# A hybrid decoder step on one core: the loads of the S5 constants moved from SyncE's order into ScalarE's

## The chip, the cores and the metric

The kernel runs on one core of a Trainium2 chip. The metric is device time in microseconds. Three runs of the kernel before gave 2245.57, 2238.49 and 2242.0 us, median 2242.0.

The engines are called by the profile's names: PE (TensorE matmul), PEld (TensorE weight load), DVE (VectorE), ACT (ScalarE), POOL (GpSimd), SP (SyncE). SP computes nothing; its instructions begin DMAs.

## The reference

One inference step of a trunk of 2 layers over a prompt of 2048 tokens, with 8 more single tokens (the "sample") through the same weights. In every layer the 1024 channels are split in four groups of 256, one a mixer: A (retention), H (gated linear recurrence), S (S5, a diagonal complex state space) and M (Mamba-2). All read one input projection, and an output projection and the residual end the layer:

```python
hn = rms_norm(x, norm_w)
proj = (hn @ w_in).astype(f32)
...
sy, s5_re, s5_im = s5_scan(u, s5_h0_re, s5_h0_im, s5_A_re, s5_A_im, s5_log_dt, s5_B_re, s5_B_im, s5_C_re, s5_C_im)
...
mixed = jnp.concatenate([o_ret, o_hgrn, o_s5, o_m2], axis=-1)
x_out = x + mixed @ w_out
```

## The kernel before, in words

**Tiling.** The prompt is cut in 4 blocks of 512 tokens. With 2 layers this makes 8 blocks, here called blocks 1 to 8 (1 to 4 are layer 0). A block's large matmuls (`gemm`, `gemm_wide`) multiply its normalised input by weight tiles of 256 KB. A weight tile goes through four engines: SP begins its load into a `wr` buffer (6 of them; lines 612 and 687), ACT makes a rounded copy in a `wh` buffer (5 of them; lines 615 and 688), DVE subtracts that copy from the raw tile for the rest (lines 616 and 689), and PE multiplies by both halves (lines 628, 633 and 695). The mixers' smaller work stands between these matmuls.

**S5.** `s5_setup` computes for each layer seven constant arrays of 512 KB in HBM, `s5c[l][0..6]`. In every block `mix_S` loads them again into `big` buffers (512 KB each; `NBIG` = 10 of them, shared with the other mixers, with the sample's work and with the gates). Eleven loads a block, 88 in all:

- `s5_load` (line 241) for arrays 0 and 1 (called `binc`) and 6 (`tcs`): 3 loads of 512 KB. Arrays 0 and 1 are read by PE's 64 matmuls of line 1420, array 6 by DVE's multiplications right behind. Eight ACT copies (line 1413) fill the other operand of line 1420, `uT`, from two transposes.
- `s5_out(0)` and `s5_out(1)` (lines 1425 and 1426): 4 loads of 256 KB each, two into `tq` and two into `cq`. PE's two groups of 32 matmuls (line 1482) read them, group 0 those of `s5_out(0)`, group 1 those of `s5_out(1)`; 12 matmuls of a large product stand between the two groups. After each group ACT copies the result out (line 1483).

In blocks 1 and 5 (`B.b` is 0) `s5_out(1)` is called after group 0, in the other blocks before it:

```python
tq, cq = nxt
if qh == 0 and B.b:
    nxt = s5_out(1)
elif qh == 1:
    if not B.b:
        tq, cq = s5_out(1)
    yield 1
```

**The sample's work.** In the second half of block 1 and 5 and the first of block 2 and 6 the 8 sample tokens go through their own mixers (class `Dec`), which use `big` buffers too. `Dec.mix_S` loads one with 16 small broadcasts a layer (line 1025, SP) and multiplies it into another (line 1030, DVE, twice).

**What sets the order.** PE's order is written out by hand: `tc.manual_schedule` keeps PE in the order in which the program is traced. On ACT, DVE, POOL and SP a scheduler of the framework sets the order when the program is built. It goes by priority, which is the position in the trace less the offset of `tc.high_priority` (the loads, casts and subtractions of weight tiles have 100, evacuations of large products 100, the sample's work minus 50), and by its own estimate of when inputs, buffers and engines are free. At run time every engine takes its instructions strictly in that order, and an instruction that begins a DMA waits in it like any other: for its buffer to be free, and for one earlier DMA to have landed (DMAs are counted on eight semaphores in turn). In the kernel before all 1284 DMAs are begun by SP.

Of the kernel before, what the change touches and what calls it, by code (L numbers as in the profile page):

```python
# [113 lines left out]
def trunk_kernel(ctx: ExitStack, tc: tile.TileContext, A: dict):  # L114
    nc = tc.nc
# [34 lines left out]
    def big(shape=(P, 1024), dt=F32):  # L150
        if alt[0] and AB[alt[0]]:
            return smp.tile(list(shape), dt, name=nm("big"), tag="big" + alt[0], bufs=AB[alt[0]])
        return bigp.tile(list(shape), dt, name=nm("big"), tag="big")
# [83 lines left out]
    s5c = [[drp.tile([P, 1024], F32, name=f"s5c{i}_{j}", tag=f"s5c{i}_{j}") for j in range(7)] for i in range(DEPTH)]  # L237

    def s5_load(l, j):
        t = big()  # L240
        nc.sync.dma_start(t, s5c[l][j])
        return t

    hA = hH = hM = None
# [1153 lines left out]
    def mix_S(L, B):  # L1398
# [5 lines left out]
        for hb in range(2):  # L1404
            ps = mbank()
            for i in range(4):
                g = hb * 8 + 2 * i
# [3 lines left out]
            for g2, sg in halves():  # L1411
                for r, sl in halves():
                    (V.tensor_copy if 2 * r + g2 in UV else S.copy)(uv[sl, :, g2, :], pv[sg, :, r, :])
        binc = [s5_load(L.l, j).rearrange("p (a q x) -> p a q x", a=2, q=4) for j in range(2)]
        yield 3
        bre, bim = mbank(), mbank()
# [5 lines left out]
        def s5_out(qh):  # L1422
            tq, cq = big([P, 2, 4, P]), big([P, 2, 4, P])
            for hb in range(2):
                nc.sync.dma_start(tq[:, hb], s5c[L.l][2 + hb][:, 512 * qh : 512 * qh + 512].rearrange("p (g x) -> p g x", g=4))
                nc.sync.dma_start(cq[:, hb], s5c[L.l][4 + hb][:, 512 * qh : 512 * qh + 512].rearrange("p (g x) -> p g x", g=4))
            return tq, cq

        tcs = s5_load(L.l, 6).rearrange("p (a q j) -> p a q j", a=2, q=8)
        tc_ = tcs[:, 0].rearrange("p q j -> p (q j)")  # L1430
        ts_ = tcs[:, 1].rearrange("p q j -> p (q j)")
# [29 lines left out]
        carry = cn  # L1461
        yield 4
        nxt = s5_out(0)
        Y = big([P, 8, P])
        yield 4
        for qh in range(2):
# [7 lines that stand above are left out]
            ps = mbank()  # L1474
            for q2 in range(2):
                for r in range(2):
                    g4 = 2 * q2 + r
                    for i in range(2):
                        for hb in range(2):
                            q = 4 * hb + 2 * qh + q2  # L1480
                            lhs = uT[:, 2 * q + r, :] if i else X[:, r, q, :]
                            T.matmul(ps[64 * hb : 64 * hb + 64, g4 * P : (g4 + 1) * P], lhs, (tq if i else cq)[:, hb, g4], start=(i == 0), stop=(i == 1))  # L1482
            S.copy(Y[:, :, qh * 64 : qh * 64 + 64].rearrange("p t (g c) -> p g t c", g=4), ps.rearrange("p (g t c) -> p g t c", g=4, c=16))
# [404 lines left out]
    for l in range(DEPTH):  # L1888
        L = Layer()
# [163 lines left out]
```

## Time and profile before

| what | value |
|---|---|
| three runs | 2245.57, 2238.49, 2242.0 us; median 2242.0 |
| the profiled execution's own time | 2245.02 us |
| its span, first to last instruction | 2243.2 us |
| mean granted TensorE clock | 0.98 of full speed |
| PE busy | 2118.9 us (94%) |
| DVE busy | 1669.3 us (74%) |
| ACT busy | 1034.2 us (46%) |
| POOL busy | 239.5 us (11%) |
| DMA | 284.41 MB, mean 127 GB/s |

The profile is one execution. "Busy" counts the engines' own work; waits and the beginning of DMAs are not in it, so SP has no busy time. A timeline row is: start in us, length in us, engine and line, operation, the tile written and the tiles read, the shapes, how many instructions were merged; in square brackets the idle time before it and what ended it. A small "q" behind an engine's name is its sequencer. A matmul's end is modelled.

### The profile page before, as it was taken

The numbers are of one execution on the slowest core, as the hardware profiler recorded it, in microseconds if no ns is written. First come the engines' busy times: TensorE is split into PE (matmuls) and PEld (weight loads), VectorE is DVE, ScalarE is ACT, GpSimd is POOL, SyncE is SP. The second block draws the span as 40 slices with busy tenths as digits, with TensorE's granted clock in tenths as the row PEclk, the third lists the DMA queues.
The fourth block names the chain that finished last, engine by engine and source line by source line (L and its number), as shares of the span: only waits on it lengthen the run. The fifth ranks groups of instructions, "written<-read, shape, count | busy, mean of one in ns | idle before, by whom it ended". The sixth has DMA issues, their size and how long they took to land. (4 is left out here: it accounts for less than half of the span.)

```text
span 2243.2 us, 41062 instructions
## 1 busy us (share of the span) xinstructions
PE 2118.9 (94%) x15031; PEld 1712.8 (76%) x15031; DVE 1669.3 (74%) x4614; ACT 1034.2 (46%) x1889; POOL 239.5 (11%) x212
## 2 busy tenths in 40 slices
PE   7999989999999999999999998999899899999996
PEld 7778767776777877788877876777677678878786
DVE  6888666898749977787747867489985687748774
ACT  7434433456333564346453453444634245454343
POOL 0112011000210002201100011000120001100100
PEclk9999999999999999999999999999999999999999
DMA  6324633236524364374533335334652253431272
GB/s 213 104 66 120 182 104 118 90 108 203 143 67 143 94 196 121 115 167 126 179 97 112 95 113 165 99 109 119 202 154 78 86 163 101 156 92 50 68 260 94
DMA packets 263354, 284.41 MB, mean 127 GB/s; under 512 B 88752, under 2 KB 183616, under 8 KB 263152
## 3 DMA queue, kind: packets, MB, share of 16 engines
q1 hardware_dynamic: 263152, 281.79, 42.4%
q8 instruction: 118, 1.93, 0.4%
q14 instruction: 84, 0.69, 0.1%
HBM read 245.52 MB, written 31.99 MB: 124 GB/s over the span
## 5 line engine op out<-in xcount | busy, mean ns | idle before, releaser
L695 PE MATMUL gb<-wh,hn 128*128 128x512 f32 x2208 | 542.1, 400 | 3.4 <-DVE half L1650 2.3
L633 PE MATMUL gb<-hn,wh 128*128 128x512 f32 x1920 | 485.9, 406 | 10.3 <-DVE wh L616 6.9
L695 PEld LDWEIGHTS gb<-wh,hn 128*128 128x128 f32 x2208 | 409.9, 188 | 109.1 <-issue 11.6
L633 PEld LDWEIGHTS gb<-hn,wh 128*128 128x128 f32 x1920 | 359.9, 192 | 99.2 <-DVE wh L616 8.1
L689 DVE TENSOR_TENSOR wh<-wr,wh 128x512 fp32r<-128x512 f32 x296 | 215.3, 732 | 242.6 <-ACT wh L688 239.2
L688 ACT CAST wh<-wr 128x512 fp32r<-128x512 f32 x296 | 183.2, 620 | 373.5 <-PE gb L695 193.6
L695 PE MATMUL gb<-wh,mx 128*128 128x512 f32 x1344 | 341.5, 407 | 7.9 <-DVE half L1733 5.8
L695 PEld LDWEIGHTS gb<-wh,mx 128*128 128x128 f32 x1344 | 251.3, 192 | 77.8 <-DVE half L1733 10.1
L615 ACT CAST wh<-wr 128x512 fp32r<-128x512 f32 (+1 forms) x248 | 152.3, 619 | 308.4 <-PE gb L633 83.5
L616 DVE TENSOR_TENSOR wh<-wr,wh 128x512 fp32r<-128x512 f32 (+1 forms) x248 | 183.3, 745 | 77.6 <-ACT wh L615 74.2
L628 PE MATMUL gb<-wh,hn 128*128 128x256 f32 (+1 forms) x1728 | 220.2, 286 | 11.1 <-DVE convc L1524 4.7
L628 PEld LDWEIGHTS gb<-wh,hn 128*128 128x128 f32 x1728 | 211.6, 191 | 15.8 <-issue 9.2
L1585 POOL TENSOR_TENSOR half<-mats,m_lal 128x512 fp32r<-128x512 f32 x64 | 75.5, 1198 | 829.1 <-DVE m_lal L1579 278.8
L1330 DVE COPY_PREDICATED big<-lvl,mb 64x256 f32<-64x256 int32 x192 | 95.3, 537 | 2.5
L1297 ACT COPY zbH<-big 64x512 f32<-64x512 f32 x112 | 70.8, 632 | 48.5 <-PE mb L1306 35.9
L1523 DVE SCALAR_TENSOR_TENSOR big<-gb,vt,big 128x511 f32<-128x511 f32 (+2 forms) x96 | 71.1, 743 | 3.9 <-ACT big L1521 3.5
L1306 PE MATMUL mb<-zbH,big 128*64 128x64 f32 x1536 | 56.9, 229 | 11.0 <-DVE half L1177 5.3
L1306 PEld LDWEIGHTS mb<-zbH,big 128*64 128x64 f32 x1536 | 50.8, 142 | 20.5 <-issue 15.4
L1281 POOL TENSOR_TENSOR big<-mats,h_dg 128x1024 f32<-128x1024 f32 x16 | 30.7, 1942 | 241.8 <-DVE h_dg L1278 197.6
L1482 PE MATMUL mb<-big,big 128*64 128x128 f32 x512 | 40.6, 307 | 15.1 <-DMA big<-s5c 14.7
L628 PE MATMUL gb<-wh,mx 128*128 128x256 f32 x384 | 47.3, 282 | 4.7 <-DVE mx L1505 2.8
L1482 PEld LDWEIGHTS mb<-big,big 128*64 128x64 f32 x512 | 33.6, 155 | 23.7 <-issue 17.0
(497 smaller groups left out, 3091.2 us busy)
## 6 DMA issues: line engine op xcount, KB each, us to landing
wr<-in_w_in SPq DMA_DIRECT2D x416, 256.0 KB
wr<-in_w_out SPq DMA_DIRECT2D x128, 256.0 KB
big<-s5c SPq DMA_DIRECT2D x64, 256.0 KB
xn<-xmid SPq DMA_DIRECT2D x32, 512.0 KB
xn<-in_x_prompt SPq DMA_DIRECT2D x24, 512.0 KB
big<-s5c SPq DMA_DIRECT2D x24, 512.0 KB
xmid<-half SPq DMA_DIRECT2D x44, 256.0 KB
half<-xmid SPq DMA_DIRECT2D x44, 256.0 KB
```

The source lines that it names most:

```text
L615: S.copy(hl[:, 0, :, :n], raw[:, :, :n])
L616: V.tensor_tensor(hl[:, 1, :, :n], raw[:, :, :n], hl[:, 0, :, :n].bitcast(F32), ALU.subtract)
L628: T.matmul(o, lhs[2 * ks[ki] + k][:, a, tt * P : (tt + 1) * P], hls[ki][:, c, k, :n], start=(ki == 0 and k == 0 and pi == 0 and tt % per = ...
L633: T.matmul(banks[i], hls[ki][:, a, k, i * P : (i + 1) * P], lhs[2 * ks[ki] + k][:, c, :], start=(ki == 0 and k == 0 and pi == 0), stop=(ki ...
L688: S.copy(hl[:, 0, 0:512], raw[:, 0:512])
L689: V.tensor_tensor(hl[:, 1, 0:512], raw[:, 0:512], hl[:, 0, 0:512].bitcast(F32), ALU.subtract)
L695: T.matmul(banks[tt], lhs[ks[kt]][:, a, tt * P : (tt + 1) * P], hls[kt][:, c, 0:512], start=(kt == 0 and pi == 0), stop=(kt == KT - 1 and ...
L1306: T.matmul(ps[su, j * 64 : (j + 1) * 64], k[:, j // 4, (j % 4) * P + 64 * u : (j % 4) * P + 64 * u + 64], qz[:, :, j * 64 + 32 * u : j * 6 ...
L1330: V.copy_predicated(stv[p][su, :, nu * u : nu * u + nu, :], mv, ps[su, p * 256 : p * 256 + 256].rearrange("p (c b h) -> p c b h", c=8, h=h))
L1482: T.matmul(ps[64 * hb : 64 * hb + 64, g4 * P : (g4 + 1) * P], lhs, (tq if i else cq)[:, hb, g4], start=(i == 0), stop=(i == 1))
L1523: V.scalar_tensor_tensor(acc[:, 3 - i :], ps[:, : TB - 3 + i], w(i), acc[:, 3 - i :], ALU.mult, ALU.add)
L1585: E('m').tensor_tensor(mms[tt][i].rearrange("p (h t) -> p h t", h=4), tri[:, None, :].to_broadcast([P, 4, P]), lal[:, i, tt, :][:, :, None ...
```

## The change

The 88 loads of `s5c` are begun by ACT (`nc.scalar`) and no longer by SP (`nc.sync`). Nothing else in the source differs; the scheduler places them anew among ACT's instructions.

```diff
 def s5_load(l, j):
     t = big()
-    nc.sync.dma_start(t, s5c[l][j])
+    nc.scalar.dma_start(t, s5c[l][j])
     return t
...
 for hb in range(2):
-    nc.sync.dma_start(tq[:, hb], s5c[L.l][2 + hb][:, 512 * qh : 512 * qh + 512].rearrange("p (g x) -> p g x", g=4))
-    nc.sync.dma_start(cq[:, hb], s5c[L.l][4 + hb][:, 512 * qh : 512 * qh + 512].rearrange("p (g x) -> p g x", g=4))
+    nc.scalar.dma_start(tq[:, hb], s5c[L.l][2 + hb][:, 512 * qh : 512 * qh + 512].rearrange("p (g x) -> p g x", g=4))
+    nc.scalar.dma_start(cq[:, hb], s5c[L.l][4 + hb][:, 512 * qh : 512 * qh + 512].rearrange("p (g x) -> p g x", g=4))
 return tq, cq
```

## Rows read from the trace of the kernel before

**Rows 1.** The page's busy times: us, share of the span, instructions.

```profile
PE 2118.9 (94%) x15031; PEld 1712.8 (76%) x15031; DVE 1669.3 (74%) x4614; ACT 1034.2 (46%) x1889; POOL 239.5 (11%) x212
```

**Rows 2.** PE's waits: who waited for what, us in total, times, longest.

```profile
PE mb L1482 <- DMA big<-s5c: 14.7, 10, 4.7
PE gb L633 <- DVE wh L616: 6.9, 2, 4.0
```

**Rows 3.** Line 1482 by itself: idle time before it, us and times.

```profile
  DMA big<-s5c: 19.8, 19
```

**Rows 4.** PE's timeline, an undisturbed group 0 in block 3.

```profile
862.61 1.97 PE L1482 MATMUL mb<-big,big 128*64 128x128 f32 x32
```

**Rows 5.** PE's timeline in block 2.

```profile
561.97 2.09 PE L1420 MATMUL mb<-big,big 128*64 128x64 f32 x64
...
592.53 4.52 PE L1482 MATMUL mb<-big,big 128*64 128x128 f32 x32 [4.67 <-DMA big<-s5c]
...
600.32 1.97 PE L1482 MATMUL mb<-big,big 128*64 128x128 f32 x32
```

**Rows 6.** PE's timeline in block 6.

```profile
1679.43 0.41 PE L1482 MATMUL mb<-big,big 128*64 128x128 f32 x2 [4.74 <-DMA big<-s5c]
...
1686.63 0.43 PE L1482 MATMUL mb<-big,big 128*64 128x128 f32 x2
```

**Rows 7.** Stretches: length, busy PE, PEld, DVE, ACT, POOL (count), PEclk, DMA share, GB/s.

```profile
552.00:562.00 10.00, 9.68 (x44) 7.19 (x44) 7.84 (x9) 5.21 (x15) 0.00 (x0) 1.00 0.84 289
...
591.00:597.80 6.80, 5.26 (x34) 4.14 (x35) 6.80 (x14) 0.59 (x1) 1.34 (x1) 0.50 0.67 218
```

**Rows 8.** SP's timeline in block 2.

```profile
587.84 0.42 SPq L1425 DMA_DIRECT2D big<-s5c  x1
588.31 0.91 SPq L1426 DMA_DIRECT2D big<-s5c  x2
...
595.32 0.80 SPq L1426 DMA_DIRECT2D big<-s5c  x2
```

**Rows 9.** SP's waits from 577 to 597 us (block 2).

```profile
SPq L687 <- DVE wh L616: 5.6, 3, 3.3
SPq L1426 <- DVE big L1030: 4.6, 1, 4.6
```

**Rows 10.** ACT's timeline in block 2: around group 0, and the copies of line 1413.

```profile
552.39 3.05 ACT L1413 COPY big<-mb 64x256 f32<-64x256 f32 x8
...
583.80 1.25 ACT L1460 COPY big<-half 64x504 f32<-64x504 f32 x2 [4.05 <-DVE half L1456]
```

**Rows 11.** PE's, SP's and ACT's timelines in block 1.

```profile
310.56 1.97 PE L1482 MATMUL mb<-big,big 128*64 128x128 f32 x32
...
316.93 0.40 PE L1482 MATMUL mb<-big,big 128*64 128x128 f32 x2 [1.43 <-DMA big<-s5c]
...
313.40 0.86 SPq L1426 DMA_DIRECT2D big<-s5c  x2
...
313.99 0.62 ACT L1483 COPY big<-mb 128x512 f32<-128x512 f32 x1
...
315.53 0.62 ACT L688 CAST wh<-wr 128x512 fp32r<-128x512 f32 x1
```

**Rows 12.** SP's timeline: the three loads of line 241 in blocks 2 and 8.

```profile
552.82 2.20 SPq L241 DMA_DIRECT2D big<-s5c  x3
...
2139.94 1.46 SPq L241 DMA_DIRECT2D big<-s5c  x3
```

**Rows 13.** ACT's and PE's timelines in block 8: copies of line 1413, and their reader.

```profile
2144.24 1.12 ACT L1413 COPY big<-mb 64x256 f32<-64x256 f32 x3
...
2149.71 2.09 PE L1420 MATMUL mb<-big,big 128*64 128x64 f32 x64
```

**Rows 14.** A load's length on SP: ns min/median/max, first and last start.

```profile
L1425 SPq DMA_DIRECT2D big<-s5c x32: 320/430/758, 268.0 to 2157.1; - x32
```

**Rows 15.** ACT's busy time over eight stretches around the S5 work of the eight blocks.

```profile
sum 487.00, ACT 207.47; mean ACT 25.93
```

## The prediction

> **What bounds the kernel now.** I read the page's busy times first: PE works 94% of the span, ACT 46% [rows 1]. PE's order is written by hand and does not change, so the change can only move PE's idle time and the time that PE's clock loses. Then I read what PE waits for: the largest single entry is this change's subject, 14.7 us in 10 waits for the S5 constants at line 1482; PE waits for weights only 6.9 us, in two places [rows 2]. With PE's weight loads the idle time before line 1482 that such a DMA ended is 19.8 us [rows 3]. That is, but for the clock, the ceiling of any gain from earlier loads, 0.9% of the span.
>
> It does not lie evenly. A group of 32 matmuls of line 1482 takes 1.97 us when its constants are there [rows 4], and so it is in blocks 3, 4, 7 and 8. Four groups lose: group 0 in blocks 2 and 6 (waits of 4.67 and 4.74 us) [rows 5, 6], and group 1 in blocks 1 and 5. A loss is more than its wait: in block 2 the group also takes 4.52 us and not 1.97. Its last loads were still landing, and the granted clock was 0.50, the lower of the two levels (1.2 GHz), in the stretch behind the wait, in which PE had been idle; before that it stood at 1.00 [rows 7].
>
> Why the loads were late differs, and that decides the change. In block 2 SP begins those of group 0 at 587.84, the moment at which PE begins to wait [rows 8]. SP's list of waits there shows none for them: it stood 5.6 us before weight loads whose buffers DVE had not freed. The two `cq` loads of group 1 did wait for a buffer, 4.6 us, until DVE's line 1030 was done [rows 9].
>
> **The change part by part.** All durations are from the profiled execution, whose own time is 2245.0 us, 3.0 above the median of the runs, 2242.0; the sum is made against 2245.0 and then set against the median. 0.3% (6.7 us) is about what a measurement of this kernel can tell from no change.
>
> *Blocks 2 and 6.* ACT has no queue of weight loads in front of the constants, and it stands idle for 4.05 us before 583.80 [rows 10]. So group 0's loads should be begun before 584 and its wait should go. In block 2 group 0 cost 4.67 + 4.52 - 1.97 = 7.2 us, in two blocks 14.4. But the next thing is late: PE would reach group 1 after group 0 and the 12 matmuls between the groups (597.05 to 600.32 now), near 593, and its `cq` buffers are freed by DVE at 595.3, which the change does not touch. From a load's begin to PE's first use I take 3.5 us, from block 1, where PE waited for it (313.40 to 316.93) [rows 11]. Group 1 then begins at 595.3 + 0.4 + 3.5 = 599.2 and not at 600.32, a gain of 1.1. In block 6 the same gate leaves about 0.9. **Minus 2 us.** Ends: 0, if ACT's order brings the loads no earlier; minus 14.4, if the scheduler's new order frees the second pair's buffer earlier too. I take the near end, since the wait for DVE stands in the rows.
>
> *Blocks 1 and 5.* Here group 1's loads wait for buffers that group 0 frees. In block 1 that ends at 312.53, and SP begins the loads that moment, the first `cq` load at 313.40. On ACT they stand behind the copy of group 0's result, which ends at 314.61 and itself follows activations. The `cq` loads then begin near 315.05, 1.65 us later, and PE waits that much longer. For two blocks 3.3, of which I take 3, since ACT's sequencer may begin a load while the copy still runs. **Plus 3 us.** Ends: minus 1, if the loads get ahead of the activations and SP's other work no longer precedes them; plus 7.2, if they also come behind the two casts that end at 316.15 (3.6 later, twice).
>
> *The three early loads of each block.* SP begins them 0.4 us after the first of the eight copies of line 1413 and 9.15 us before PE's line 1420 needs them [rows 5, 10, 12]. On ACT they come behind the copies, 2.6 us later. DMA moves 289 GB/s in such a stretch [rows 7], so a load's further 256 KB take 0.9 us; the second load, begun 0.45 after the first, should be there 0.45 + 3.5 + 0.9 = 4.9 us after the first begins. 2.6 + 4.9 is less than 9.15, so it stays hidden; the other blocks but the last lie alike. In block 8 the copies end only at 2145.36, 5.4 us behind SP's begin, and 2145.4 + 4.9 = 2150.3 against line 1420 at 2149.71, whose second half reads it half a microsecond later [rows 12, 13]. **Plus 1 us** for what my estimate may be short. Ends: 0 and plus 6 (a microsecond and a half more in the tight blocks, with a spell of the low clock).
>
> *ACT's time and SP's.* A load takes SP 0.43 us [rows 14]; 88 of them put 38 us into ACT's order, 4.7 a block. The rows before show no DMA begun by ACT, so its price there is SP's. Cover: in eight stretches around this work ACT is busy 207 of 487 us, so 280 are free [rows 15]. What is behind the loads are casts of weights, then DVE's subtraction, then PE, and the five `wh` buffers between let ACT be some microseconds late; if that cover is gone, PE pays. I let 5% through: **plus 2 us**; ends 0 and 8 (a fifth). SP is rid of the same 38 us, but PE waits for SP's weights only in the 6.9 us above, which I leave as they are: 0. POOL begins no DMA. A load on ACT may also wait for the landing of a DMA that SP begins eight places earlier; I count that inside the upper end.
>
> On the price of a load: the rows show SP's alone, 0.32 to 0.76 us. The Trainium skill, Perfetto Trace Analysis, section DMA Instruction — HWDGE (DVE, Sync), says that the sequencers share one descriptor generator and that each must lock it. By it ACT and SP would at times wait for each other, and as an estimate from that page the term could double and the sum be plus 6. No row here has two sequencers that begin DMAs, so the trace is silent.
>
> *The scheduler.* All but PE's order is planned anew. PE's idle time other than for the constants is 2243.2 - 2118.9 - 14.7 = 109.6 us; a new plan can shift it either way. Value 0, ends minus 8 and plus 8.
>
> Sum: -2 + 3 + 1 + 2 = +4, so 2249 against the profiled execution and **2246 us** against the median.
>
> **The rivals.** *SP's queue was the whole matter (faster).* The constants come early everywhere, block 2 and 6 get their 14.4 us back, and the clock stays up. For it: SP's list has no wait for those loads but 5.6 us for others. Against: the wait for DVE behind it. With the other terms at half, 2242 - 14 + 2 = 2230 us. It decides if the new plan lets group 1's `cq` loads begin before 593.
>
> *ACT's order delays the constants (slower).* One mechanism: a load stands behind ACT work that needs nothing of it. It decides where a load comes more than about 2 us later than on SP: blocks 1 and 5, and block 8's early loads. Price: 7.2 + 6, and 4 from delayed casts, less 1 from blocks 2 and 6: 2242 + 16 = 2258 us. For it: ACT is busy without a gap from the activations to 316.15 in block 1. Against: elsewhere ACT idles more than half of the time.
>
> *Nothing moves.* The loads are begun when their buffers come free, as before, whoever begins them: 2242 us. The Trainium skill, DMA: Bandwidth & Descriptors, section Issuing engines are not separate DMA queues, says that beginning DMAs on several engines saves only the time to initiate them. By that rule no landing gets shorter; it leaves out that SP stood in line before it began, which the trace does show. I count this case to no change.
>
> **How the numbers follow.** No change within 0.3% (my forecast at 2246, and the last rival): 0.40. Faster by more: 0.27, for the first rival and for a lucky plan. Slower by more: 0.33, for the second and for an unlucky plan. I hold slower for likelier than faster since the gate in blocks 2 and 6 stands in rows, and the loss in 1 and 5 too. The range reaches a little beyond both rivals, 2228 to 2264; about 2 in 10 stay outside.
>
> **What would show it.** In the changed profile: begins of `s5c` by ACT, and none by SP. Group 0 of blocks 2 and 6 without a wait, and instead a wait for the constants before their group 1, ended near the landing of `cq` behind DVE's line 1030. Group 1 of blocks 1 and 5 waiting 1 to 2 us longer. No wait at line 1420, or a small one in block 8. ACT's waits for weights and DVE's waits for casts about as before. I am wrong if group 1 in blocks 2 and 6 has no wait, if line 1420 waits in several blocks, or if PE waits for weights in new places.

## The result and the profile after

The changed kernel took 2261.3 us (median of 4 runs, 2256.88 to 2264.1), the kernel before beside it 2241.2 us (4 runs, 2238.49 to 2245.57). The ratio is 1.0084, 95% interval [1.0063, 1.0104]: slower, by about 20 us. The forecast was 2246 us and no change; the time lies inside the range, and near the price of the slower rival, 2258.

The profiled execution has its own time of 2264.1 us and a span of 2262.0 us, 18.8 more than before. The page's busy times, to be read beside [rows 1]:

```profile
PE 2123.1 (94%) x15031; PEld 1716.8 (76%) x15031; DVE 1674.1 (74%) x4614; ACT 1034.9 (46%) x1889; POOL 237.1 (10%) x212
```

PE's waits, as in [rows 2]:

```profile
PE mb L1482 <- DMA big<-s5c: 29.0, 10, 11.1
...
PE gb L633 <- DVE wh L616: 6.4, 2, 3.5
```

The span splits in three: PE's busy time, its wait for the constants, and the rest. Before: 2118.9 + 14.7 + 109.6. After: 2123.1 + 29.0 + 109.9. So 14.3 of the 18.8 us are waits for the constants, 4.2 are matmuls that took longer (the mean granted clock was 0.974 and not 0.980), and all other idle time is the same to 0.3 us. PE's timeline says where, in blocks 2 and 6 (start, length; idle time before it in brackets):

```profile
563.35 2.09 PE L1420 MATMUL mb<-big,big 128*64 128x64 f32 x64
...
600.24 0.66 PE L1482 MATMUL mb<-big,big 128*64 128x128 f32 x2 [11.10 <-DMA big<-s5c]
601.52 3.99 PE L1482 MATMUL mb<-big,big 128*64 128x128 f32 x30 [0.62 <-DMA big<-s5c]
...
608.96 1.97 PE L1482 MATMUL mb<-big,big 128*64 128x128 f32 x32
...
1664.70 2.09 PE L1420 MATMUL mb<-big,big 128*64 128x64 f32 x64
...
1701.25 0.66 PE L1482 MATMUL mb<-big,big 128*64 128x128 f32 x2 [10.68 <-DMA big<-s5c]
...
1709.14 1.97 PE L1482 MATMUL mb<-big,big 128*64 128x128 f32 x32
```

Group 0 waits 11.10 us where it waited 4.67 [rows 5], and 10.68 where it waited 4.74 [rows 6]. From line 1420 to group 1 block 2 takes 45.6 us instead of 38.35, block 6 44.4 instead of 37.8 (line 1420 stood at 1648.85 there): 13.9 us in two places. The granted clock fell in the wait and stayed down behind it; columns as in [rows 7], the first stretch is the wait of block 2, the second the group behind it, at the lower level (1.2 GHz):

```profile
589.10:600.20 11.10, 0.04 (x1) 0.00 (x0) 9.63 (x19) 2.10 (x5) 3.41 (x4) 0.68 0.75 213
600.20:606.60 6.40, 5.69 (x35) 4.40 (x36) 1.91 (x6) 1.03 (x2) 0.00 (x0) 0.50 0.89 321
```

Why the loads came late stands in ACT's timeline in block 2:

```profile
552.00 0.33 ACTq L241 DMA_DIRECT2D big<-s5c  x1
...
553.75 1.14 ACT L1413 COPY big<-mb 64x256 f32<-64x256 f32 x3
554.53 0.33 ACTq L241 DMA_DIRECT2D big<-s5c  x1
554.90 1.89 ACT L1413 COPY big<-mb 64x256 f32<-64x256 f32 x5
...
560.24 0.62 ACT L688 CAST wh<-wr 128x512 fp32r<-128x512 f32 x1 [2.61 <-PE gb L695]
560.64 0.33 ACTq L241 DMA_DIRECT2D big<-s5c  x1
...
594.05 0.26 ACT L999 ACTIVATE junk<-half 32x64 bf16<-32x64 f32 x1 [3.80 <-DVE half L997]
594.06 0.33 ACTq L1425 DMA_DIRECT2D big<-s5c  x1
...
594.43 0.44 ACTq L1426 DMA_DIRECT2D big<-s5c  x1
```

The loads of group 0 begin at 594.06, behind an instruction of the sample's work that stood 3.80 us for DVE; SP began them at 587.84 [rows 8]. And work that the diff doesn't name is later too. Three of its instructions on DVE and SP, first before, then after: X's first column (line 1449), the last of the 16 broadcasts (line 1025) and its reader (line 1030).

```profile
562.13 0.17 DVE L1449 COPY big<-s_carry 64x8 f32<-64x8 f32 x1
...
574.64 2.19 SPq L1025 DMA_DIRECT2D big<-pd_su  x3
...
590.55 1.21 DVE L1030 TENSOR_TENSOR big<-big,bb 128x1024 f32<-128x1024 f32 x1
```

```profile
576.73 2.81 DVE L1449 COPY big<-s_carry 64x8 f32<-64x8 f32 x4
...
588.81 4.24 SPq L1025 DMA_DIRECT2D big<-pd_su  x6
...
596.05 1.23 DVE L1030 TENSOR_TENSOR big<-big,bb 128x1024 f32<-128x1024 f32 x1 [1.43 <-DMA big<-pd_su]
```

### The profile page after: what moved, and what is told of

It reads as the page before. It is cut to its first block, busy times and chain, and to the rows that moved or that the text cites. A ratio compares the mean times of both kernels' runs of the same rounds, so it can differ in the third digit from the quotient of the medians.

```text
span 2262.0 us, 41045 instructions
## 1 busy us (share of the span) xinstructions
PE 2123.1 (94%) x15031; PEld 1716.8 (76%) x15031; DVE 1674.1 (74%) x4614; ACT 1034.9 (46%) x1889; POOL 237.1 (10%) x212
## 5 line engine op out<-in xcount | busy, mean ns | idle before, releaser
L695 PEld LDWEIGHTS gb<-wh,hn 128*128 128x128 f32 x2208 | 411.1, 189 | 109.6 <-issue 11.5
L616 DVE TENSOR_TENSOR wh<-wr,wh 128x512 fp32r<-128x512 f32 (+1 forms) x248 | 178.7, 725 | 78.3 <-ACT wh L615 75.0
L1306 PEld LDWEIGHTS mb<-zbH,big 128*64 128x64 f32 x1536 | 51.3, 143 | 19.4 <-issue 14.7
```

The lines of the kernel that those rows point to most:

```text
L616: V.tensor_tensor(hl[:, 1, :, :n], raw[:, :, :n], hl[:, 0, :, :n].bitcast(F32), ALU.subtract)
L695: T.matmul(banks[tt], lhs[ks[kt]][:, a, tt * P : (tt + 1) * P], hls[kt][:, c, 0:512], start=(kt == 0 and pi == 0), stop=(kt == KT - 1 and ...
L1306: T.matmul(ps[su, j * 64 : (j + 1) * 64], k[:, j // 4, (j % 4) * P + 64 * u : (j % 4) * P + 64 * u + 64], qz[:, :, j * 64 + 32 * u : j * 6 ...
```

## The experiments

Four theories stood at the start. **1**: the loads of `s5_out` stand in ACT's order behind instructions that wait for DVE. **2**: array 6 comes late on ACT and DVE's S5 work with it. **3**: beginning 88 loads costs ACT time that its casts lack. **4**: an unlucky new plan. All runs below were timed beside the kernel before, whose median was 2241.9 us in the first set, 2244.3 in the second and 2243.8 in the third.

### Which loads, which blocks

`e1_out_only` and `e1_early_only` move one half of the loads each:

```diff
 # e1_out_only: the kernel after, but
-    nc.scalar.dma_start(t, s5c[l][j])
+    nc.sync.dma_start(t, s5c[l][j])
 # e1_early_only: the kernel after, but, in s5_out
-    nc.scalar.dma_start(tq[:, hb], ...)
-    nc.scalar.dma_start(cq[:, hb], ...)
+    nc.sync.dma_start(tq[:, hb], ...)
+    nc.sync.dma_start(cq[:, hb], ...)
```

> Only the 64 loads of s5_out (lines 1425, 1426) are begun by ACT; the 24 of line 241 are begun by SP again. Theory 1 (in blocks 2 and 6 the loads of group 0 stand in ACT's order behind ACT instructions that wait for DVE; PE waits 11 us there, not 4.7): the loss stays, 2254 to 2262 us, PE's longest waits at line 1482 near 11 us. Theory 2 (line 241's array 6 comes late on ACT in blocks 2 and 6, so DVE's S5 work and all behind it is late): the loss goes, 2241 to 2247 us. Theory 3 (what counts is the number of loads that ACT has to begin): 64 of 88, so about 2255 us, spread over all blocks.

> Only the 24 loads of line 241 are begun by ACT; the 64 of s5_out are begun by SP again. Theory 1: near the kernel before, 2240 to 2246 us, waits at line 1482 back at 4.7 us. Theory 2: most of the loss, 2252 to 2262 us. Theory 3: 24 of 88, about 2247 us.

Measured: `e1_out_only` 2254.3 us, ratio 1.0056 [1.0034, 1.0077], longest wait at line 1482 3.1 us. `e1_early_only` 2261.9 us, 1.0090 [1.0068, 1.0111]. The 24 early loads alone cost as much as the whole change, with the same two waits, although SP begins the loads that PE waits for. PE's and SP's rows of `e1_early_only`:

```profile
602.31 3.02 PE L1482 MATMUL mb<-big,big 128*64 128x128 f32 x20 [10.60 <-DMA big<-s5c]
...
591.58 3.97 SPq L1025 DMA_DIRECT2D big<-pd_su  x6
...
597.22 0.42 SPq L1425 DMA_DIRECT2D big<-s5c  x1
```

`e1_out_only` took a time that theories 1 and 3 both allow, but without the waits of 11 us that theory 1 named. Theory 1 as it stood falls, and so does 3 for the early loads (it gave 2247). The two halves, 12 and 20 us, add up to more than the whole.

`e1_b26_back` and `e1_b26_only` go by block (`B.b` is 1 in blocks 2 and 6), for all eleven loads of a block:

```diff
 # e1_b26_back; e1_b26_only has the two engines exchanged
-    nc.scalar.dma_start(...)
+    (nc.sync if B.b == 1 else nc.scalar).dma_start(...)
```

> All loads are begun by ACT except those of blocks 2 and 6 (22 loads), which SP begins. Theories 1 and 2 (the place is blocks 2 and 6): 2240 to 2247 us, waits of group 0 there near 4.7 us. Theory 3: 66 of 88 loads are left on ACT, about 2256 us. A new plan of the scheduler as the cause (theory 4) names no number; it would show as a loss with no wait for the constants.

> Only the 22 loads of blocks 2 and 6 are begun by ACT, all others by SP. Theories 1 and 2: the loss of the whole change, 2254 to 2262 us, with waits of about 11 us before group 0 of blocks 2 and 6. Theory 3: 22 of 88, about 2246 us.

Measured: `e1_b26_back` 2251.5 us, 1.0032 [1.0015, 1.0048]; `e1_b26_only` 2258.0 us, 1.0066 [1.0043, 1.0089], with waits of 10.76 and 10.72 us. Most of the loss is made in blocks 2 and 6, as theories 1 and 2 said; but 7 us by the ratio stay when these two are put back, more than the 2240 to 2247 us expected. In that profile the wait is 15.6 us and the rest 109.5, so what is left lies in PE's busy time, 2125.4 against 2118.9; a single profile doesn't show why (see the last section).

### The order in which buffers are handed out

What do arrays 0 and 1 have to do with buffers needed 40 us later? In block 2 of the built programs (the traces name no buffer numbers), the buffers of group 0 are those that arrays 0 and 1 leave when line 1420 ends (564.06 before, 565.44 after); nothing else uses them until the loads 24 and 29 us later. So neither a buffer nor a transfer held the loads, but their place in the plan; and a higher priority for the call (offsets of 100 to 1000; built and not run) left their place in SP's order in blocks 2 and 6 as it was. That gave **theory 5**: the scheduler hands out the ten buffers of `big` in the order in which the tiles are traced. The order here is arrays 0 and 1, array 6, X (line 1449), the sample's two tiles (lines 1025 and 1030), and only then group 0. In three of the four profiles of the first set the loads of group 0 begin 1.4 to 2.7 us ahead of line 1030, as in the kernels before (2.7) and after (2.0).

> Only arrays 0 and 1 of line 241 (16 loads) are begun by ACT; array 6 and s5_out by SP. Theory 5 (the buffers of big are handed out in the order in which the tiles are traced; a load of arrays 0 and 1 placed among ACT's eight copies makes every later tile of that queue later in the plan: X, the sample's two tiles of lines 1025 and 1030, and only then the buffers of group 0): the whole loss, 2253 to 2263 us, waits of 10 to 11 us before group 0 of blocks 2 and 6 although SP begins those loads. Theory 2 (array 6 is what comes late): no loss, 2240 to 2246.

> Only array 6 of line 241 (8 loads) is begun by ACT. Theory 5: 2240 to 2247 us, waits before group 0 of blocks 2 and 6 near 4.7 us. Theory 2: 2252 to 2262 us with waits near 10.6 us.

```diff
 # e2_binc: the kernel before, but (e2_tcs has the two engines exchanged)
-    nc.sync.dma_start(t, s5c[l][j])
+    (nc.sync if j == 6 else nc.scalar).dma_start(t, s5c[l][j])
```

Measured: `e2_binc` 2259.6 us, 1.0070 [1.0054, 1.0086], waits of 10.37 and 10.67 us; `e2_tcs` 2246.3 us, 1.0012 [1.0001, 1.0023], waits of 5.20 and 4.82. Theory 2 falls; 16 loads make nearly the whole loss.

The next pair takes one tile out of the queue. It needs no wait to be removed: the sample's product gets a buffer of its own.

```diff
-            pr = big([P, 8, 8, 16])
+            pr = smp.tile([P, 8, 8, 16], F32, name=nm("dpr"), tag="dpr", bufs=1)
```

> The kernel after, but the sample's product tile of line 1030 has a buffer of its own and is no longer one of the ten of big. Theory 5: the loads of group 0 in blocks 2 and 6 no longer stand behind it; they are begun some 15 us earlier, the two waits of 11 us go and group 1's buffer is free as well: 2261 less 14 to 28 = 2233 to 2247 us. Theory 1 (ACT's waits for DVE in front of the loads are the cause, whatever the buffers): the loads still come behind them and at most half of it is won, 2250 to 2262 us.

> The kernel before with the same buffer of its own for the tile of line 1030; all loads on SP. Theory 5: the waits of 4.7 us before group 0 in blocks 2 and 6 go, with the slow groups behind them: 2242 less up to 14.4 = 2228 to 2236 us. If the weight loads on SP in front were the cause (as the prediction had it), the waits stay near 4.7 us and the time is 2239 to 2245.

Measured: with the change 2243.6 us, 0.9993 [0.9981, 1.0006], as theory 5 had it; without it 2226.6 us, 0.9926 [0.9909, 0.9943], **faster than both kernels** and a little below the 2228 expected. SP's and PE's timelines of `e2_before_own_tile` in block 2:

```profile
561.51 0.34 SPq L1425 DMA_DIRECT2D big<-s5c  x1
...
587.05 1.97 PE L1482 MATMUL mb<-big,big 128*64 128x128 f32 x32
...
591.93 1.97 PE L1482 MATMUL mb<-big,big 128*64 128x128 f32 x32
```

And its list of PE's waits:

```profile
PE mb L1482 <- DMA big<-s5c: 6.1, 6, 2.2
```

SP begins the same loads at 561.51 and not at 587.84, and both groups of block 2 run in 1.97 us without a wait. One tile of another computation, standing ahead in the queue, had held them; SP's weight loads, which are all still there, had not.

### What else the move costs

Theory 5 does not explain why the two kernels of that pair differ by 17 us. The third set asks.

> The kernel after, with the two loads of arrays 0 and 1 traced ahead of the two transposes and the eight copies of line 1413 (they are still begun by ACT, and their buffers stand ahead of the copies' tile in the queue of big). Theory 5: most of the loss goes, since X, the tile of line 1025 and that of line 1030 are handed out at their old times again: 2240 to 2250 us, waits before group 0 of blocks 2 and 6 of 5 us or less. If it is ACT's beginning 88 loads that costs (theory 3): 2256 to 2264.

```diff
 # the kernel after; ahead of the loop with the transposes and the copies of line 1413
+        binc = [s5_load(L.l, j).rearrange("p (a q x) -> p a q x", a=2, q=4) for j in range(2)]
...
 # behind that loop
-        binc = [s5_load(L.l, j).rearrange("p (a q x) -> p a q x", a=2, q=4) for j in range(2)]
```

Measured: 2254.2 us, 1.0040 [1.0024, 1.0057]. A miss, by half: group 0 of block 2 no longer waits, but group 1 behind it waits 5.78 us, and group 0 of block 6 still 9.06.

> The kernel after with the buffer of its own for line 1030's tile, and arrays 0 and 1 begun by SP again; array 6 and the 64 loads of s5_out stay on ACT. Theory 5 alone (place of arrays 0 and 1, nothing else): like the kernel before with that buffer, 2224 to 2232 us. If the 64 loads of s5_out on ACT have a price of their own, as their run alone (2254 against 2242) suggests (theory 3b): 2234 to 2242.

```diff
 # the kernel after with the buffer for pr, and
-    nc.scalar.dma_start(t, s5c[l][j])
+    (nc.scalar if j == 6 else nc.sync).dma_start(t, s5c[l][j])
```

Measured: 2246.1 us, 1.0001 [0.9985, 1.0017]. With all loads on SP the ratio was 0.9926: 17 us by the ratios (19.5 by the medians) are missing, outside both expectations; theory 5 alone fails. Between the two profiles lie 22.8 us. PE waits 5.6 us for the constants, 0.5 less than in `e2_before_own_tile`; the rest of the idle time is 118.3 us (2247.0 - 2123.1 - 5.6) against 109.1; and PE's busy time is 2123.1 against 2109.0, so the largest part, 14.1 us, is one that these profiles don't explain. For the idle time, the timelines of ACT and DVE show where some of it comes from in blocks 2 and 6, and PE's what came of it:

```profile
563.73 0.33 ACTq L1425 DMA_DIRECT2D big<-s5c  x1
...
564.64 0.33 ACTq L1425 DMA_DIRECT2D big<-s5c  x1
568.43 1.02 ACTq L1426 DMA_DIRECT2D big<-s5c  x2
569.55 3.90 ACTq L1425 DMA_DIRECT2D big<-s5c  x2
573.54 0.62 ACT L615 CAST wh<-wr 128x512 fp32r<-128x512 f32 x1 [8.92 <-DMA big<-s5c]
...
574.20 0.69 DVE L616 TENSOR_TENSOR wh<-wr,wh 128x512 fp32r<-128x512 f32 x1 [3.49 <-ACT wh L615]
...
1658.13 0.62 ACT L615 CAST wh<-wr 128x512 fp32r<-128x512 f32 x1 [6.62 <-DMA big<-pd_su]
...
1684.34 0.59 ACT L1483 COPY big<-mb 128x512 f32<-128x512 f32 x1 [7.29 <-DVE dpr L1030]
...
601.41 3.91 PE L633 MATMUL gb<-hn,wh 128*128 128x512 f32 x9 [4.22 <-DVE half L930]
...
1684.98 3.68 PE L1482 MATMUL mb<-big,big 128*64 128x128 f32 x32 [3.77 <-ACT big L1483]
```

Six loads, four of them begun between 568.43 and 573.45, stand in front of a cast of weights. They wait, and the cast stands 8.92 us behind them, in block 6 another 6.62. In block 2 DVE stands 3.49 us for that cast, its second instruction of line 1030 comes 2.4 us later behind line 1420 than in `e2_before_own_tile` (597.50 - 563.62 against 592.67 - 561.22), and PE waits 4.22 us where it waits 1.14 there:

```profile
595.93 2.36 PE L633 MATMUL gb<-hn,wh 128*128 128x512 f32 x9 [1.14 <-DVE half L930]
```

In block 6 DVE stands only 0.98 us for the cast. PE's 3.77 us are a wait for ACT's copy of line 1483, which stood until DVE's line 1030 was done; why group 1 waits for that copy here, and not in `e2_before_own_tile`, is not settled. `e2_before_own_tile` in turn waits 1.32 us before line 633 in block 6, which this kernel doesn't. So the two places make 5.5 of the 9.2 us by which the idle times differ.

In `e1_out_only` a cast stood 9.37 us for another release: the load in front of it waited for its buffer, which line 1030 left at 600.93. The name in the bracket is the last event, line 1031; the load shows the true one. ACT's timeline:

```profile
600.97 0.81 ACTq L1426 DMA_DIRECT2D big<-s5c  x2
601.82 0.44 ACTq L1425 DMA_DIRECT2D big<-s5c  x1
602.36 0.62 ACT L615 CAST wh<-wr 128x512 fp32r<-128x512 f32 x1 [9.37 <-DVE half L1031]
```

> All 88 loads are begun by GpSimd, whose order has no copies of line 1413 and few waits for DVE. Theory 5: the plan of the sample's tiles stays as in the kernel before, so 2238 to 2248 us with waits near 4.7 us before group 0 of blocks 2 and 6. If leaving SP is what costs, whoever takes the loads: 2255 to 2262.

```diff
 # in s5_load and s5_out of the kernel after
-    nc.scalar.dma_start(...)
+    nc.gpsimd.dma_start(...)
```

Measured: 2259.2 us, 1.0069 [1.0043, 1.0095], inside the other expectation. The one from theory 5 fails: the sample's tiles are back near their old times (first broadcast 562.33), yet group 0 waits 8.87 and 7.60 us. POOL's timeline and PE's in block 2:

```profile
591.55 1.04 POOL L1133 TENSOR_TENSOR half<-half,half 128x256 f32<-128x256 f32 x1 [0.86 <-ACT wh L615]
592.55 1.77 POOL L1134 TENSOR_TENSOR half<-half,half 128x256 f32<-128x256 f32 x1
594.27 0.59 POOL L1425 DMA_DIRECT2D big<-s5c  x1
...
598.79 0.66 PE L1482 MATMUL mb<-big,big 128*64 128x128 f32 x2 [8.87 <-DMA big<-s5c]
```

The loads stand behind elementwise work of lines 1133 and 1134 that follows DVE and PE. So theory 1 comes back beside 5, for an engine with work of its own.

> The kernel before; the call of s5_out(0) stands ahead of the yield, so that its two buffers come ahead of the sample's in the queue, with no further buffer. All loads on SP. Theory 5: faster than before, 2226 to 2236 us, no wait before group 0 in blocks 2 and 6, perhaps one before group 1. If the queue of buffers is not the cause: 2239 to 2246.

```diff
 # the kernel before
-        yield 4
         nxt = s5_out(0)
+        yield 4
```

Measured: 2240.0 us, 0.9983 [0.9965, 1.0]. By its time this run belongs to the other expectation. The trace says more: group 0 of blocks 2 and 6 no longer waits, so the order of the queue does decide when those loads begin (theory 5), but group 1 now waits 5.25 and 5.56 us: with the same ten buffers the wait moves one group on. The further buffer for `pr`, 512 KB, is what pays.

## Why the prediction was right and where it was wrong

**The time** lies inside the range, 3 us from its end, and that is luck: the end was set a little beyond a rival whose mechanism is not what cost the time. The forecast, no change, was wrong, and the likeliest case had the wrong sign in its main term.

**Blocks 2 and 6: the step that failed.** Put as "ACT has no queue of weight loads in front of the constants, and it stands idle for 4.05 us before 583.80. So group 0's loads should be begun before 584." The term was -2, ends 0 and -14.4; measured, from line 1420 to group 1, +7.3 and +6.7. Two errors. First, the loads were late before not because SP stood behind weight loads but because their buffers come after the sample's tile in the queue (`e2_before_own_tile`); the 5.6 us of [rows 9] were true and beside the point. Second, an idle stretch was read as free time. The 4.05 us of [rows 10] are a wait in a strict order: whatever stands behind it starts no earlier. The end of 0 shut out a loss with no row to support that. The next gate named, the `cq` loads behind line 1030, existed: in the new trace ACT begins them at 600.29, with the end of line 1030 at 600.26.

**Blocks 1 and 5: sign right, the step itself did not happen.** Taken +3, with the loads behind the activations and the copy of group 0's result. ACT's sequencer began them between the activations, while the engine computed: in block 1 three of the four ahead of that copy (312.44, 312.80 and 313.33; the copy at 314.03), in block 5 all four, and the first 0.06 us after group 0's end in both. The waits at line 1482 grew all the same, by 0.3 us in block 1 (2.15 to 2.46) and 0.8 in block 5 (2.71 to 3.50), about 1 us and not 3; why these loads landed later is not settled. The upper end takes 3.6 us a block from the first load; for the `cq` loads, by which the value goes, it would be 3.2 (316.15 + 0.44 - 313.40).

**The three early loads: right where I looked, wrong in what they touch.** Line 1420 never waits for a DMA, so the cost at the reader is 0. The room was smaller than written: blocks 1 and 5 don't lie like block 2, since there the copies end 5.3 and 5.6 us behind SP's begin, which with the 4.9 us leaves less than 0.3 us; and ACT began the loads among the copies, not behind them. But `e2_binc` shows that the loads of arrays 0 and 1, begun by ACT among its copies, bring a plan in which all later tiles of the queue are late: 15.4 us (2259.6 - 2244.3). The step counted the direct reader alone. Why the scheduler's estimates then put X's first columns behind the scans (562.13 to 576.73) is not settled.

**ACT's time: the price right, the danger elsewhere.** A load of line 1425 takes ACT 0.33 us in the median and one of line 1426 0.44, against SP's 0.43 for either [rows 14], and PE waits 6.4 us for weights against 6.9: in the kernel after the term of +2 is about 0. (ACT's busy time, 1034.9 against 1034.2, says nothing of it: the beginning of DMAs is not in it.) What a load can cost ACT is the time it stands for a buffer, with the casts behind it (9.37 us in `e1_out_only`), and that was not in the sum. The Trainium skill, Perfetto Trace Analysis, section DMA Instruction — HWDGE (DVE, Sync), draws the issuing sequencer as waiting for semaphores, then for a lock. The casts that stood 8.92 and 6.62 us agree with the first; a doubled price from the lock does not show in the 0.33 us.

**The scheduler's new plan**: value 0, ends -8 and 8. Outside the constants PE's idle time moved by 0.3 us (109.6 to 109.9). The plan did matter, but through the loads' place.

**The rivals.** "ACT's order delays the constants", at 2258, came nearest (2261.3), but not by its mechanism: blocks 1, 5 and 8 were named and blocks 2 and 6 decided, and there no ACT work in front of the loads is needed, since in `e1_early_only` SP begins group 0's loads and the loss is the same. "SP's queue was the whole matter" fell with `e2_before_own_tile`. "Nothing moves" fell too. The Trainium skill, DMA: Bandwidth & Descriptors, section Issuing engines are not separate DMA queues, has beginning on several engines save only sequencer time; here moving them cost 20 us. The order of the engine that begins a DMA decides when it may begin (group 0's loads behind a wait of 3.80 us on ACT), and through the plan when other work comes.

**Open:** `e1_out_only` costs 12 us, of which its profile shows 8.4: 5.4 in PE's busy time, 0.6 in the wait for the constants, 2.4 elsewhere. How much of the first answers to the casts and how much to the clock's own spread was not separated. The same holds for the 17 us between `e3_own_tile_binc_sp` and `e2_before_own_tile`: that the 64 loads of `s5_out` (with array 6) cost something on ACT stands in the medians, what of it is the casts behind waiting loads does not. Nor do the costs add up: the two halves of the change cost 12 and 20 us, the whole 20.

## What to carry to other kernels

Before a load is moved to another engine, ask what it waits for: when its buffer stood free and no transfer held it, it is its place in a plan, and the cure is there (here one tile out of a shared pool, for 512 KB more of buffer: -17.7 us). An engine that is idle in a trace may be waiting in a strict order, as ACT was here, and a DMA put behind that wait waits too; a DMA that must wait for a buffer holds up everything behind it on an engine that also computes. And when buffers go out in the order of tracing, count the cost of a late load for every later tile of that pool, not for its reader alone.

## What the runs showed of the hardware

ACT begins DMAs while it computes: in block 1 of the kernel after, a load begins at 312.44 inside an activation that runs from 312.11 to 312.71.

```profile
312.11 0.60 ACT L1242 ACTIVATE big<-gb 128x512 f32<-128x512 f32 x1
312.44 0.33 ACTq L1425 DMA_DIRECT2D big<-s5c  x1
```

On GpSimd a load is work of the engine itself: 0.56 us in the mean for line 1425, and POOL's busy time rose from 239.5 [rows 1] to 287.8 us, 48.3 for 88 loads.

Two executions of one order differ by microseconds through the clock. In `e1_b26_only` all engines have the order of the kernel before until about 538 us; by then PE is 5.5 us late, as the same matmuls of line 1632 show: up to there it was busy 499.7 us against 493.4, and idle 0.8 us less. PE's timeline, first of the kernel before, then of `e1_b26_only`:

```profile
533.27 0.69 PE L1632 MATMUL mb<-half,half 128*64 128x64 f32 x16 [0.60 <-DVE m_rs L229]
```

```profile
538.73 0.69 PE L1632 MATMUL mb<-half,half 128*64 128x64 f32 x16 [0.52 <-DVE m_rs L229]
```

And one stretch, columns as in [rows 7], in the same order of kernels:

```profile
374.00:379.00 5.00, 5.00 (x23) 4.05 (x23) 1.83 (x4) 0.62 (x1) 3.77 (x2) 1.00 0.04 13
```

```profile
374.00:379.00 5.00, 5.00 (x22) 4.20 (x22) 0.73 (x3) 0.10 (x1) 3.36 (x2) 0.66 0.20 63
```

PE is busy all of the time in both, yet the granted clock is 1.00 in one and 0.66, a mean of the two levels, in the other. What PE did just before was the same, a wait of 0.31 us at line 1164. So a difference of 5 us in PE's busy time between two single profiles, like the 4.2 us above, proves little alone; the waits and the medians carry the argument.
